# A state-space mixer whose running sums are loaded to all partitions from DRAM in place of a matmul with a triangle

## The chip, the cores and the metric

The kernel runs on one core of a Trainium2 chip. Its metric is the device time of one execution in microseconds (us). Five engines have queues of their own: PE (matmul; PEld is its weight load), DVE (VectorE), ACT (ScalarE), POOL (GpSimd) and SP (SyncE), which here issues nearly all DMAs. Each queue works strictly in order.

## The reference

Two layers of a diffusion trunk over 1024 latent and 128 context tokens, 1152 in all and thus nine blocks of 128. In each layer one projection feeds four mixers (state-space, neighbourhood attention, RWKV-7, differential attention); an output projection and an MLP follow. Only the state-space mixer is changed. For each head h, each direction and each block (chunk) of 128 tokens it computes

```python
la = (dt * A)                                   # 8 numbers per token: 2 directions x 4 heads
cs = jnp.cumsum(la, axis=-1)                    # running sums over the 128 tokens of the block
seg = jnp.where(tri, cs[..., :, None] - cs[..., None, :], -jnp.inf)
lmat = jnp.exp(seg).astype(dtype)
gmat = jnp.einsum('bclhn,bcshn->bhcls', Cc, Bc) * lmat
y_diag = jnp.einsum('bhcls,bcshp->bclhp', gmat, xdt)
```

So each block needs, for each of its eight (direction, head) pairs, a 128 x 128 tile cs[l] - cs[s]: cs[s] is a scalar per partition, and cs[l] is a row that must stand on all 128 partitions.

## The kernel before

Features lie on partitions, tokens along the free axis. The input projection is a row of calls of `proj` (feature-major, three chunks of 384 tokens, each chunk a product of 24 matmuls, three per k) and `proj_tm` (token-major, a product of 24 matmuls per block). Every large product is made of three fp32r matmuls per k (L99, L100, L101, in `mm3`), into PSUM tiles `psd` of which there are two.

In a layer the code is written in this order (L1477 to L1516): `proj` for the state-space mixer's four tiles and `proj_tm` for its z and dt; then `ssd` (the state-space mixer, L414); then nine further `proj` (the inputs of RWKV) and `proj_tm` for the values of the neighbourhood attention (its evacuations are L282, its stores to DRAM L283, its last store L287); then `rwkv_prep` (L595), which convolves the nine RWKV tiles and writes them back to DRAM; then `rwkv_open` and the first part of RWKV (`rwkv_first`, L777, called u00 here); then, in the pool `qk`, eight `proj_qk` and one more `proj_tm`.

The framework lists the instructions of each engine by a schedule of its own, by readiness and by priority: `rwkv_prep` has priority 1000, so its instructions are put as early as their data and their memory allow. Tiles come from pools that lie as stacks from the left and the right end of a partition's memory. A new pool that lies on the bytes of an older one waits until the older one's tiles are done with. The pools that matter:

- `sd_big` and `sd_tmp`, left: the tiles of `ssd`. They are given back when `ssd` is done.
- `rp`, left, right above `sd_tmp`: the tiles of `rwkv_prep` (`u` twice, `x0` to `x3`, each 1152 wide, `st` twice).
- `stg`, right: three buffers `st` of 384 columns, through which every `proj` and `proj_tm` goes to DRAM up to L287.
- `m1`, right, layer 0 only: the tiles of the modulation (`mod`, `junk`), a sum by DVE that runs beside the projections.
- `qk`, right, opened after `rp` is closed; it lies on the bytes of `rp`. `proj_qk` evacuates its products to it.

Within `ssd` the loop over blocks (L527) makes for each direction d a PSUM tile `cp`: for each head the column la of the block, broadcast to 128 columns, times the triangle `ctri[d]` (L560), which puts the running sums on all partitions. DVE subtracts the block's own sums from it into `Md` (L563), ACT takes the exponential (L565), DVE multiplies with the products of B and C (L566), and PE multiplies with the inputs (L572). PSUM tiles of `ssd` come from three buffers (`psr` twice, `psx`).

Before the loop the same running sums of all blocks and directions are already made once, as rows of 72 partitions (`cr`, L477 to L480); they are transposed to `cs`, the scalars per partition.

Of the kernel before, what the change touches and what calls it, by code (L numbers as in the profile page):

```python
# [8 lines left out]
F32 = mybir.dt.float32  # L9
# [10 lines left out]
NB = T // 128  # L20
# [14 lines left out]
def bcast_in(ap, n):  # L35
    return ap.unsqueeze(len(ap.shape)).to_broadcast(list(ap.shape) + [n])
# [58 lines left out]
def mm3(nc, ps, pairs):  # L95

    n = len(pairs)
    for i, ((ah, al), (bh, bl)) in enumerate(pairs):
        nc.tensor.matmul(ps, al, bh, start=i == 0, stop=False)  # L99
        nc.tensor.matmul(ps, ah, bh, start=False, stop=False)  # L100
        nc.tensor.matmul(ps, ah, bl, start=False, stop=i == n - 1)  # L101


def psd(env):

    env.turn += 1
    if env.wide and env.turn % 3 == 0:
        return psx(env)
    return ps2(env)
# [18 lines left out]
def psr(env):  # L128

    env.turnr += 1  # L130
    if env.turnr % 3 == 0:
        return psx(env)
    return env.ps_r.tile([128, 512], F32, tag="r", name="psr")
# [156 lines left out]
def residual(env, x, kt, c0, n, ps, g):  # L290
    for a0, m, cd in STREAMS:
        s0, s1 = max(a0, c0), min(a0 + m, c0 + n)
        if s1 > s0:
            env.nc.vector.scalar_tensor_tensor(out=x[:, kt, s0:s1], in0=ps[:, s0 - c0:s1 - c0], scalar=g[:, kt, cd:cd + 1],  # L294
                                               in1=x[:, kt, s0:s1], op0=ALU.mult, op1=ALU.add)
# [16 lines left out]

def out_proj(env, A, L, x, M, k0, g, first, xd=None):

    nc = env.nc
    nk = 6 - k0 if first else len(M)
    W = {}
    lo = k0 * 128

    def product(kt, c0, n):  # L320
        h, l = W[kt]
        ps = psd(env)
        mm3(nc, ps[:, :n], [((h[:, i * 128:i * 128 + 128], l[:, i * 128:i * 128 + 128]), (M[i][0][:, c0:c0 + n], M[i][1][:, c0:c0 + n])) for i in range(nk)])
        residual(env, x, kt, c0, n, ps, g)


    m = env.wcol // (nk * 128)
    order = []
    for a in range(0, 8, m):
        b = min(8, a + m)  # L330
        raw = env.wp.tile([128, env.wcol], F32, tag="raw", name="raw", bufs=1)[:, 0:(b - a) * nk * 128]
        nc.sync.dma_start(out=raw.rearrange("p (k x) -> p k x", k=b - a), in_=A["w_out"][L, a:b, :, lo:lo + nk * 128].rearrange("k p x -> p k x"))
        h, l = split(env, raw)
        for k in range(a, b):
            W[k] = h[:, (k - a) * nk * 128:(k - a + 1) * nk * 128], l[:, (k - a) * nk * 128:(k - a + 1) * nk * 128]
        if first:
            if a == 0:
                M = M()

            for k in (0, 1) if a == 0 else range(a + 1, min(b + 1, 8)):  # L340
                nc.vector.tensor_copy(x[:, k, 0:1], (l if a else M[-1][1])[:, 0:1].bitcast(F32))
                nc.sync.dma_start(out=x[:, k], in_=xd[:, k])
            for k in range(a, b):
                for c0, n in CH3:
                    product(k, c0, n)
    if not first:
        for c0, n in CH3:
            for kt in range(8):
                product(kt, c0, n)
# [64 lines left out]
def ssd(env, ctx, src, zdt, par, rows, st0, yout, stout):  # L414
    tc, nc, C = env.tc, env.nc, env.const
    big = ctx.enter_context(tc.tile_pool(name="sd_big", reuse_waits="tile", bufs=1))
    tp = ctx.enter_context(tc.tile_pool(name="sd_tmp", reuse_waits="tile", bufs=2))
    PS = lambda: psr(env)
# [4 lines left out]
    ctri, ctri2 = [t[:, 0], t[:, 1]], t.rearrange("p a b -> p (a b)")  # L423
    nc.vector.tensor_scalar_mul(out=pt[:, 0:24], in0=pt[:, 0:24], scalar1=0.5)
    xt = big.tile([128, NB, 256], F32, name="xt")
    x = [None, None]
# [45 lines left out]
    la = big.tile([128, NB, 8], F32, name="la")  # L472
    nc.vector.scalar_tensor_tensor(out=la, in0=dt, scalar=-1.0, in1=bcast_mid(eA, NB), op0=ALU.mult, op1=ALU.mult)

    cs = big.tile([128, NB, 8], F32, name="cs")
# [2 lines left out]
    nc.tensor.matmul(pc[:, 0:72], C.ones, f(la), start=True, stop=True)  # L478
    cr = tp.tile([72, 256], F32, tag="ze", name="cr")
    nc.scalar.activation(out=cr, in_=pr[0:72, 0:256], func=AF.Copy)  # L480
    for d in range(2):
        nc.tensor.transpose(pq[:, d * 72:d * 72 + 72], cr[:, d * 128:d * 128 + 128], C.ident[0:72, 0:72])
    for d in range(2):
# [12 lines left out]
    h4 = lambda a: a.rearrange("p (h x) -> p h x", h=4)  # L496
# [30 lines left out]
    for b in range(NB):  # L527
        zt = tp.tile([128, 256], F32, tag="zt", name="zt")
        nc.sync.dma_start(out=zt, in_=zdt[:, b, 0:256])
        ze = tp.tile([128, 256], F32, tag="ze", name="ze")  # L530
        nc.scalar.activation(out=ze, in_=zt, func=AF.Tanh, scale=0.5)
        nc.vector.tensor_scalar(out=ze, in0=ze, scalar1=0.5, scalar2=0.5, op0=ALU.mult, op1=ALU.add)
        nc.gpsimd.tensor_tensor(out=zt, in0=zt, in1=ze, op=ALU.mult)

        gp = [PS(), PS()]
        for g in range(2):
            w = slice(g * 64, g * 64 + 64)
            cb = x[3][w, b * 128:b * 128 + 128]
            nc.tensor.matmul(gp[g][:, 0:128], x[2][w, b * 128:b * 128 + 128], cb, start=True, stop=True)
            for d in range(2):  # L540
                nc.tensor.matmul(gp[g][:, 128 + d * 128:256 + d * 128], cb, Sin[w, d, b], start=True, stop=True)
        Gm = []
        for d in range(2):
            G = tp.tile([128, 256], F32, tag="Gm", name="Gm")
            for g in range(2):
                nc.vector.tensor_tensor(out=G[:, g * 128:g * 128 + 128], in0=gp[g][:, 0:128], in1=ctri[d], op=ALU.mult)
            Gm.append(G)
        t = tp.tile([128, 512], F32, tag="t", name="t")
        t4 = t.rearrange("p (d g h x) -> p d g h x", d=2, g=2, h=2)
        for g in range(2):  # L550
            for d in range(2):
                nc.vector.tensor_tensor(out=t4[:, d, g], in0=gp[g][:, 128 + d * 128:256 + d * 128].rearrange("p (h x) -> p h x", h=2),
                                        in1=bcast_in(ecs[:, b, d * 4 + g * 2:d * 4 + g * 2 + 2], 64), op=ALU.mult)
        M = []
        xd = tp.tile([128, 2, 256], F32, tag="xd", name="xd")
        for d in range(2):
            nc.gpsimd.tensor_tensor(out=h4(xd[:, d]), in0=h4(xt[:, b]), in1=bcast_in(dt[:, b, d * 4:d * 4 + 4], 64), op=ALU.mult)
            cp = PS()
            for h in range(4):
                nc.tensor.matmul(cp[:, h * 128:h * 128 + 128], la[:, b, d * 4 + h:d * 4 + h + 1].to_broadcast([128, 128]), ctri[d], start=True, stop=True)  # L560
            Md = tp.tile([128, 512], F32, tag="Md", name="Md")
            for h in range(4):
                nc.vector.tensor_scalar(out=Md[:, h * 128:h * 128 + 128], in0=cp[:, h * 128:h * 128 + 128], scalar1=cs[:, b, d * 4 + h:d * 4 + h + 1], scalar2=0.0,  # L563
                                        op0=ALU.subtract, op1=ALU.min)
            nc.scalar.activation(out=Md, in_=Md, func=AF.Exp)  # L565
            nc.vector.tensor_tensor(out=Md.rearrange("p (g h l) -> p g h l", g=2, h=2), in0=Md.rearrange("p (g h l) -> p g h l", g=2, h=2),  # L566
                                    in1=Gm[d].rearrange("p (g l) -> p g l", g=2).unsqueeze(2).to_broadcast([128, 2, 2, 128]), op=ALU.mult)
            M.append(Md)
        yp = PS()
        for h in range(4):  # L570
            for d in range(2):
                nc.tensor.matmul(yp[:, h * 64:h * 64 + 64], M[d][:, h * 128:h * 128 + 128], xd[:, d, h * 64:h * 64 + 64], start=d == 0, stop=d == 1)  # L572
        y = tp.tile([128, 256], F32, tag="y", name="y")
        nc.gpsimd.tensor_tensor(out=h4(y), in0=h4(xt[:, b]), in1=bcast_in(rb[:, 16:20], 64), op=ALU.mult)
        nc.gpsimd.tensor_tensor(out=t[:, 0:256], in0=t[:, 0:256], in1=t[:, 256:512], op=ALU.add)
        nc.gpsimd.tensor_tensor(out=y, in0=y, in1=t[:, 0:256], op=ALU.add)
        nc.vector.tensor_tensor(out=y, in0=y, in1=yp[:, 0:256], op=ALU.add)
        nc.gpsimd.tensor_tensor(out=xt[:, b], in0=y, in1=zt, op=ALU.mult)
        nc.scalar.activation(out=t[:, 0:256], in_=xt[:, b], func=AF.Square, accum_out=ss[:, 0, b:b + 1])
# [804 lines left out]
def kernel(ctx: ExitStack, tc: tile.TileContext, A: dict, O: dict):  # L1384
# [54 lines left out]
    for L in range(DEPTH):  # L1439
# [40 lines left out]
        proj_tm(env, A["w_in_tm"][L, 0], H, 264, zdt)  # L1480
        sx = ExitStack()
        ssd(env, sx, PF[0:4], zdt, A["ssd_par"][L], A["ssd_rows"][L], A["st_ssd"][L], Y[0:2], O["st_ssd"][L])
        for j in (10, 11, 12, 6, 4, 8, 7, 5, 9):
            proj(j)
# [248 lines left out]
```

## Time and profile before

| what | us |
|---|---|
| median of 3 runs (lowest to highest) | 4233.19 (4231.91 to 4238.97) |
| the profiled execution, its own time | 4236.38 |
| its span, first to last instruction | 4234.6 |
| PE busy in the span | 4062.3 (96%) |
| DVE busy | 2498.9 (59%) |
| ACT busy | 1524.2 (36%) |
| POOL busy | 1104.4 (26%) |

Start with the share of PE: it is busy for nearly the whole span, so what matters is where it works, where it idles, and what it would do instead. A layer's part of interest lies at 180 to 660 us (layer 0) and at 2275 to 2720 us (layer 1). The timelines and the chain of waits are read by start time; the lines name the place in the code. A busy time of PE counts the pipelined matmuls with their drains, so that the step from one start to the next, and not the length of a record, is what one matmul costs. One fp32 matmul leaves two records.

### The profile page before, as it was taken

How to read it: one execution, taken by the hardware profiler on the slowest of the kernel's cores; microseconds unless marked ns; L12 is line 12 of the kernel's file. 1: busy time of each engine (PE TensorE's matmuls, PEld its weight loads, DVE VectorE, ACT ScalarE, POOL GpSimd, SP SyncE). 2: the span in 40 equal slices, each digit the busy share in tenths (PEclk: the TensorE clock that was granted, in tenths of full speed). 3: DMA queues.
4: the chain of work that ended last, by engine and by line, in shares of the span. 5: the costliest groups of instructions: out<-in, count | busy, mean ns of one | idle time of the engine just before them, and what ended most of it. 6: DMA issues, size and time to landing. Idle time of an engine off the chain costs nothing.

```text
span 4234.6 us, 69159 instructions
## 1 busy us (share of the span) xinstructions
PE 4062.3 (96%) x27394; PEld 3722.1 (88%) x27394; DVE 2498.9 (59%) x5734; ACT 1524.2 (36%) x2896; POOL 1104.4 (26%) x866
## 2 busy tenths in 40 slices
PE   8899889999989999999999999899999999999999
PEld 5889877777779999999998998778777999999999
DVE  4896747678675894333345756576877463333333
ACT  4333325556553212211243233355566241111111
POOL 2243340223133221111232433302322331211111
PEclk9999989989999999999999998999889999999999
DMA  6663343322221451111134333543221301111111
GB/s 196 199 199 112 121 133 76 84 64 68 54 96 54 145 169 60 40 46 40 41 110 147 119 127 95 143 97 83 41 60 46 135 26 40 43 42 40 45 41 70
DMA packets 222707, 375.74 MB, mean 89 GB/s; under 512 B 100960, under 2 KB 155760, under 8 KB 221360
## 3 DMA queue, kind: packets, MB, share of 16 engines
q1 hardware_dynamic: 222320, 371.31, 29.2%
q8 instruction: 216, 3.54, 0.4%
q14 instruction: 107, 0.88, 0.1%
q0 software_dynamic: 64, 0.02, 0.0%
HBM read 285.33 MB, written 86.42 MB: 88 GB/s over the span
## 4 chain that ended last, share of the span: by engine, by line
PE 77%; DVE 11%; DMA 5%; issue 2%; SPq 2%; ACT 2%; POOL 1%; DVEq 0%; ACTq 0%; POOLq 0%
PE psd L101 12%; PE psd L99 12%; PE psd L100 12%; PE tps L1141 5%; PE psx L101 5%; PE psx L99 5%; PE psx L100 5%; PE tps L1129 3%; PE S L1347 2%; DVE junk L162 2%; PE psd L938 1%; DVE tm L867 1%; PE psd L958 1%; PE psd L930 1%; DMA K<-scr 1%
## 5 line engine op out<-in xcount | busy, mean ns | idle before, releaser
L84 POOL TENSOR_TENSOR wl<-raw,wh 128x1024 fp32r<-128x1024 f32 (+3 forms) x200 | 474.2, 2372 | 1543.1 <-ACT wh L82 1520.5
L82 ACT ACTIVATE wh<-raw 128x1024 fp32r<-128x1024 f32 (+3 forms) x200 | 205.9, 1031 | 793.8 <-PE psd L101 672.7
L294 DVE SCALAR_TENSOR_TENSOR x<-psd,md,x 128x384 f32<-128x384 f32 (+2 forms) x442 | 212.5, 504 | 349.5 <-PE psd L101 346.0
L101 PE MATMUL psd<-fl,wh 128*128 128x384 f32 x992 | 335.2, 338 | 0.0
L99 PE MATMUL psd<-fh,wl 128*128 128x384 f32 x992 | 334.7, 337 | 0.0
L100 PE MATMUL psd<-fh,wh 128*128 128x384 f32 x992 | 334.6, 337 | 0.0
L99 PE MATMUL psd<-h2h,wl 128*128 128x384 f32 x816 | 283.5, 348 | 9.1 <-ACT st L262 6.2
L1141 PE MATMUL tps<-pT,V 128*64 128x128 f32 (+1 forms) x2144 | 287.8, 284 | 4.5 <-ACT pT L1136 3.7
L100 PE MATMUL psd<-h2h,wh 128*128 128x384 f32 x816 | 282.7, 347 | 0.0
L101 PE MATMUL psd<-h2l,wh 128*128 128x384 f32 x816 | 281.3, 346 | 0.0
L1141 PEld LDWEIGHTS tps<-pT,V 128*64 128x64 f32 (+1 forms) x2144 | 239.1, 141 | 36.2 <-issue 22.8
L379 DVE TENSOR_TENSOR fl<-s,fh 128x384 fp32r<-128x384 f32 x192 | 209.1, 1090 | 97.4 <-ACT fh L378 97.0
L1136 ACT ACTIVATE pT<-tps 128x512 f32<-128x512 f32 (+3 forms) x368 | 166.3, 475 | 173.6 <-PE tps L1129 160.6
L99 PE MATMUL psd<-h0h,wl 128*128 128x384 f32 x592 | 207.5, 350 | 0.8 <-ACT qx L1098 0.6
L377 DVE SCALAR_TENSOR_TENSOR s<-psd,r 128x384 f32<-128x384 f32 x128 | 71.2, 556 | 231.2 <-ACT r L376 230.8
L99 PE MATMUL psd<-h1h,wl 128*128 128x384 f32 x592 | 205.3, 347 | 2.4 <-ACT h1h L244 2.0
L100 PE MATMUL psd<-h0h,wh 128*128 128x384 f32 x592 | 204.9, 346 | 0.0
L100 PE MATMUL psd<-h1h,wh 128*128 128x384 f32 x592 | 204.3, 345 | 0.0
L101 PE MATMUL psd<-h0l,wh 128*128 128x384 f32 x592 | 203.8, 346 | 0.0
L101 PE MATMUL psd<-h1l,wh 128*128 128x384 f32 x592 | 202.2, 343 | 0.1
L294 DVE SCALAR_TENSOR_TENSOR x<-psx,md,x 128x384 f32<-128x384 f32 (+2 forms) x198 | 103.4, 538 | 160.6 <-PE psx L101 160.2
L1353 ACT ACTIVATE e<-e,st 128x1280 f32<-128x1280 f32 x144 | 180.5, 1253 | 47.4 <-DVE st L1352 40.6
(613 smaller groups left out, 11021.3 us busy)
## 6 DMA issues: line engine op xcount, KB each, us to landing
raw<-in_w_ff_dram SPq DMA_DIRECT2D x128, 512.0 KB
mod<-in_w_mod_dram SPq DMA_DIRECT2D x80, 512.0 KB
raw<-in_w_in_fm_dram SPq DMA_DIRECT2D x42, 512.0 KB
scr<-st SPq DMA_DIRECT2D x78, 192.0 KB
scr<-x SPq DMA_DIRECT2D x26, 576.0 KB
K<-scr SPq DMA_DIRECT2D x32, 352.0 KB
K<-scr SPq DMA_DIRECT2D x64, 176.0 KB
u<-scr SPq DMA_DIRECT2D x18, 576.0 KB
```

Of the source, the lines that this page charges most:

```text
L82: nc.scalar.activation(out=h[:, :n], in_=raw, func=AF.Copy)
L84: nc.gpsimd.tensor_tensor(out=l[:, :n], in0=raw, in1=h[:, :n].bitcast(F32), op=ALU.subtract)
L99: nc.tensor.matmul(ps, al, bh, start=i == 0, stop=False)
L100: nc.tensor.matmul(ps, ah, bh, start=False, stop=False)
L101: nc.tensor.matmul(ps, ah, bl, start=False, stop=i == n - 1)
L162: nc.vector.scalar_tensor_tensor(out=junk, in0=w[:, i * 512:i * 512 + 512], scalar=0.5, in1=parts[c * 2 + i], op0=ALU.mult, op1=ALU.mult, ...
L294: env.nc.vector.scalar_tensor_tensor(out=x[:, kt, s0:s1], in0=ps[:, s0 - c0:s1 - c0], scalar=g[:, kt, cd:cd + 1], in1=x[:, kt, s0:s1], op0 ...
L379: nc.vector.tensor_tensor(out=fl[j][:, c0:c0 + n], in0=s, in1=fh[j][:, c0:c0 + n].bitcast(F32), op=ALU.subtract)
L1129: nc.tensor.transpose(pp[0:n, i * 128:i * 128 + 128], e[:, o:o + n], C.ident)
L1136: nc.scalar.activation(out=pT[0:g[i][1], i * 128:j * 128], in_=pp[0:g[i][1], i * 128:j * 128], func=AF.Copy)
L1141: nc.tensor.matmul(out, V[0:n, vb], parts[k // 4][0:n, k % 4 * 128:k % 4 * 128 + 128], start=k == 0, stop=k == len(kt) - 1)
L1353: nc.scalar.activation(out=e[:, :N], in_=e[:, :N], func=AF.Exp, scale=-1.0, bias=m, accum_out=st[:, 6:7] if c else s0)
```

## The change

The rows `cr` of running sums, which are there already, are stored to a DRAM tile `crd`, and each block loads its eight rows of 128 sums from it, broadcast to all 128 partitions, in two DMAs (one per direction) into a tile `cb`. The matmuls of L560 and their PSUM tile are gone. The subtraction works in place on `cb`, which then takes the part of `Md`. `Md` was a tile of 512 columns with two buffers, one tile per direction; `cb` is a tile of 2 x 512 columns with two buffers, one tile per block.

```diff
     cr = tp.tile([72, 256], F32, tag="ze", name="cr")
     nc.scalar.activation(out=cr, in_=pr[0:72, 0:256], func=AF.Copy)
+    crd = env.dram([NB, 8, 256])
+    nc.sync.dma_start(out=crd.rearrange("b x l -> (b x) l"), in_=cr)
...
         M = []
+
+        cb = tp.tile([128, 2, 512], F32, tag="Md", name="cb")
+        for d in range(2):
+            nc.sync.dma_start(out=h4(cb[:, d]), in_=crd[b, d * 4:d * 4 + 4, d * 128:d * 128 + 128].unsqueeze(0).to_broadcast([128, 4, 128]))
...
-            cp = PS()
+            Md = cb[:, d]
             for h in range(4):
-                nc.tensor.matmul(cp[:, h * 128:h * 128 + 128], la[:, b, d * 4 + h:d * 4 + h + 1].to_broadcast([128, 128]), ctri[d], start=True, stop=True)
-            Md = tp.tile([128, 512], F32, tag="Md", name="Md")
-            for h in range(4):
-                nc.vector.tensor_scalar(out=Md[:, h * 128:h * 128 + 128], in0=cp[:, h * 128:h * 128 + 128], scalar1=cs[:, b, d * 4 + h:d * 4 + h + 1], scalar2=0.0,
+                nc.vector.tensor_scalar(out=Md[:, h * 128:h * 128 + 128], in0=Md[:, h * 128:h * 128 + 128], scalar1=cs[:, b, d * 4 + h:d * 4 + h + 1], scalar2=0.0,
                                         op0=ALU.subtract, op1=ALU.min)
```

The tile doubles `Md`'s memory: `sd_tmp` grows by 4096 bytes per partition, and everything above it on the left moves up. In the built program before, `rp` ends at byte 118,776, and `stg` begins at byte 121,440. After, `rp` ends at byte 122,872, so its last tiles lie on the first buffer of `stg`.

The order of instructions moves with it. Line numbers after are three higher than before from `rwkv_prep` on. On the SP queue of layer 0 before, the parameters of `rwkv_prep` (`rpar`) and its first two tiles (`u`) stand among the stores of the projections (L263) and ahead of the first weights of the neighbourhood values:

```order
L525 DMA out_st_ssd_dram<-fin 128x128 x2
L263 DMA scr_198<-st 128x384
L159 DMA mod<-in_w_mod_dram 128x1024
L263 DMA scr_198<-st 128x384 x2
L599 DMA rpar<-in_rw_par_dram 128x41
L606 DMA u<-scr_201 128x1152
L606 DMA u<-scr_202 128x1152
L91 DMA raw<-in_w_in_tm_dram 128x1024
L263 DMA scr_196<-st 128x384
L529 DMA zt<-scr_212 128x256
```

After, the same loads (L602, L609) stand behind the last store of the neighbourhood values (L287), which is the last reader of `stg`:

```order
L283 DMA scr_213<-st 128x256
L287 DMA out_nat_v_dram<-st 128x256
L91 DMA raw<-in_w_in_fm_dram 128x1024
L602 DMA rpar<-in_rw_par_dram 128x41
L609 DMA u<-scr_201 128x1152
L609 DMA u<-scr_202 128x1152
L91 DMA raw<-in_w_in_fm_dram 128x1024
L609 DMA u<-scr_203 128x1152
L619 DMA scr_221<-x_3397 128x1152
```

So the whole of `rwkv_prep` has moved behind the projections and behind `ssd`; layer 1 has the same order. On PE of layer 0 before, the small products of `rwkv_prep` (L633, L662, L651) stand one by one among the projections' matmuls, as here:

```order
L99 MATMUL psd<-wh,h1l 128x256
L633 MATMUL psm<-pack,sq 128x2 x9
L560 MATMUL psr<-ctri,la 128x128 x4
L100 MATMUL psd<-wh,h1h 128x256
L560 MATMUL psr<-ctri,la 128x128 x4
L101 MATMUL psd<-wl,h1h 128x256
```

After, all of them (L636, L654, L665) and the products of u00 (L794, L804, L813, L848) stand in one unbroken stretch, behind the first two chunks of the first `proj_qk` and ahead of its third (the last row here); L794 stands just ahead of the first row:

```order
L804 MATMUL psr<-pack,lw 128x130 x3
L636 MATMUL psm<-pack,sq 128x2 x9
L804 MATMUL psr<-pack,lw 128x130 x3
L804 MATMUL psx<-pack,lw 128x130 x3
L813 MATMUL psr<-adn,up 128x384 x2
L813 MATMUL psx<-adn,up 128x384
L665 MATMUL psm<-pack,st 64x128 x18
L654 MATMUL psm<-x_3427,pack 128x384 x3
L848 MATMUL psr<-A,B 64x64 x32
L848 MATMUL psx<-A,B 64x64 x4
L636 MATMUL psm<-pack,sq 128x2 x9
L665 MATMUL psm<-pack,st 64x128 x18
```

What was spread over the projections is now in one piece between two products of the same `proj_qk`. On the SP queue the loads of `qk` (`qkpar`) have kept their place behind the last store of `rwkv_prep` (`bo`).

## Rows read from the trace of the kernel before

**Rows 1.** chain of waits, layer 1, 2270 to 2530 us: start us, us, what

```profile
...
2347.10 0.89 PE psx L560 x8
2348.34 2.12 PE psm L662 x36
...
2403.53 2.23 PE psm L633 x18
...
2428.05 1.94 PE psm L651 x6
...
```

**Rows 2.** instructions of line 560: ns min/median/max, first and last start

```profile
...
L560 PE MATMUL psr<-ctri,la x192: 270/275/421, 265.9 to 2462.5; 128*128 128x128 f32 x192
...
L560 PE MATMUL psx<-ctri,la x96: 270/275/376, 255.6 to 2465.3; 128*128 128x128 f32 x96
...
```

**Rows 3.** windows of layer 1: PE, PEld, DVE, ACT, POOL busy; PEclk, DMA share, GB/s

```profile
...
2420.00:2500.00 80.00, 80.00 (x578) 77.30 (x578) 40.95 (x106) 27.06 (x64) 29.90 (x27) 1.00 0.34 117
...
```

**Rows 4.** timeline of the SP queue, layer 0: start us, us, what

```profile
...
269.01 0.42 SPq L599 DMA_DIRECT2D rpar<-in_rw_par_dram  x1
...
374.34 0.32 SPq L616 DMA_DIRECT2D scr<-bo  x1
...
379.32 0.42 SPq L287 DMA_DIRECT2D out_nat_v_dram<-st  x1
...
```

**Rows 5.** timeline of the SP queue, layer 1, first load of rwkv_prep

```profile
...
2277.94 0.32 SPq L606 DMA_DIRECT2D u<-scr  x1
...
```

**Rows 6.** timeline of ACT, layer 1, the same load

```profile
...
2281.80 1.25 ACT L609 ACTIVATE x<-u,rpar 128x1152 f32<-128x1152 f32 x1 [4.47 <-DMA u<-scr]
...
```

**Rows 7.** timeline of DVE, layer 1, first convolution and one step of rsqrt

```profile
...
2283.09 1.99 DVE L611 SCALAR_TENSOR_TENSOR x<-u,rpar,x 128x1023 f32<-128x1023 f32 x2 [0.75 <-ACT x L609]
2285.00 1.89 DVE L612 SCALAR_TENSOR_TENSOR x<-u,rpar,x 128x1023 f32<-128x1023 f32 x2
...
2340.25 0.18 DVE L45 SCALAR_TENSOR_TENSOR st<-st 128x18 f32<-128x18 f32 x1
...
```

**Rows 8.** groups of DVE, 268 to 460 us: busy us, mean ns, idle before

```profile
...
L641 DVE SCALAR_TENSOR_TENSOR nk<-x,rnk,psm 128x384 f32<-128x384 f32 x6 | 3.6, 605 | 1.6 <-PE psm L662 1.6
...
L652 DVE TENSOR_TENSOR bo<-x,psm 128x384 f32<-128x384 f32 x6 | 3.2, 547 | 1.1 <-PE psm L651 1.0
...
L645 DVE SCALAR_TENSOR_TENSOR x<-x,rpar,x 128x1152 f32<-128x1152 f32 x2 | 2.8, 1402 | 0.0
...
L792 DVE TENSOR_TENSOR lw<-psr,w0b 128x384 f32<-128x384 f32 x2 | 1.1, 558 | 4.8 <-PE psr L791 4.7
...
```

**Rows 9.** groups of DVE, 2698 to 2716 us

```profile
...
L850 DVE TENSOR_TENSOR B<-a,k 128x1152 f32<-128x1152 f32 x1 | 1.4, 1387 | 0.0
...
L848 DVE TENSOR_TENSOR Ti<-psr,pack 64x512 f32<-64x512 f32 x2 | 1.4, 688 | 0.0
...
```

**Rows 10.** instructions of tile D: ns min/median/max, first and last start, forms

```profile
...
L868 DVE TENSOR_REDUCE D<-tm x248: 136/416/1152, 472.4 to 3076.5; 72x1 f32<-72x1 f32 x4, 72x3 f32<-72x9 f32 x4, 72x5 f32<-72x25 f32 x4, 72x7 f32<-72x49 f32 x4
...
```

**Rows 11.** chain of waits, layer 0, 180 to 470 us

```profile
...
427.37 1.53 PE psr L791 x12
...
```

**Rows 12.** groups of PE, 2698 to 2716 us

```profile
...
L845 PE MATMUL psr<-A,B 64*64 64x64 f32 x40 | 2.2, 297 | 0.0
...
```

**Rows 13.** timeline of PE, layer 0: two matmuls of a projection, nine apart

```profile
...
253.81 0.34 PE L100 MATMUL psd<-h0h,wh 128*128 128x384 f32 x1
...
255.39 0.34 PE L100 MATMUL psd<-h1h,wh 128*128 128x384 f32 x1
...
```

**Rows 14.** windows of PE, layer 0: busy, PEclk, DMA share, GB/s

```profile
...
308.00:312.00 4.00, 4.00 (x19) 0.50 0.49 157
...
```

**Rows 15.** waits of PE, 460 to 680 us: us in total, times, longest

```profile
...
PE psm L1066 <- DVE qf L1059: 10.7, 3, 5.6
...
```

**Rows 16.** instructions of line 563

```profile
...
L563 DVE TENSOR_SCALAR Md<-psr,cs x96: 334/341/351, 270.2 to 2467.5; 128x128 f32<-128x128 f32 x96
...
```

**Rows 17.** DMA packets in 2698 to 2716 us

```profile
...
DMA packets 4021, 4.05 MB, mean 225 GB/s; under 512 B 3316, under 2 KB 3316, under 8 KB 4018
...
```

## What the change was predicted to do

> **What bounds the kernel now.** I read the page's busy shares first, then the table of windows over the two stretches in which `ssd` stands, then the chain of waits there, then the timelines of SP, ACT and DVE for `rwkv_prep`. In the windows the reader is to see that PE does not rest while `ssd` and `rwkv_prep` run: in 2420 to 2500 us it is busy for all 80 us [rows 3]. The chain there runs through PE, and the products that the change removes are links of it: a group of four running-sum products (eight records) holds it for 0.89 us [rows 1]. `rwkv_prep`, though, is no link as a whole: it hides. In layer 0 its parameters are asked for at 269.01 us and its last store (`bo`) goes out at 374.34, ahead of the last store of the neighbourhood values at 379.32 [rows 4]. So PE has projections to do for as long as `rwkv_prep` lasts, and its end meets the end of the projections. That coincidence is what the change touches.
>
> **The products removed.** L560 left 192 + 96 = 288 records [rows 2], 36 groups of eight, 18 per layer. At 0.89 us each that is 32 us of PE in all, 16 per layer. PE is the bound there, so I take all of it as a gain, before what follows.
>
> **The edits that I cost at nothing.** The store of `cr` and the first loads of `cb` stand before the loop, with the chunk states of nine blocks still to be made on PE. The later loads of `cb` wait for the products of the block two before, and the projections fill PE in between; they cost nothing while the pair lands before its block's turn. The trace has no such load. Nearest are two rows: a 576 KB load reaches ACT 3.86 us after its issue (2281.80 less 2277.94) [rows 5, 6], and in 2698 to 2716 us, where the engines of DMA were never idle, 4021 packets took 18 us, 72 ns of one of 16 engines each [rows 17]; the 512 rows of 512 bytes in a 256 KB load would be 2.3 us. If nothing hid a pair once in two blocks, it would cost 3.86 + 2 x 2.3 = 8.5 us, four times a layer, 34 us per layer; the other end is zero, and I take zero, because of the two buffers, and keep 34 for the upper end. The subtraction took 0.34 us from PSUM [rows 16]; from SBUF, in place, I cannot see it being slower, and DVE is half idle in layer 1 (40.95 of 80 us) [rows 3]: nothing.
>
> The Trainium skill ("DMA: Bandwidth & Descriptors", section Bandwidth) speaks against such loads: it wants 1 MiB or more per DMA for three quarters of the peak. Its fit of a fixed 2.0 us plus bytes over 436 GB/s (SWDGE there, SP here) would give an estimate of 2.6 us for a 256 KB load and 5.2 for a pair in a row, against 8.5 from the rows; by either I leave the term at zero, and no run here shows such a load yet.
>
> **What is moved: `rwkv_prep`.** This is the term that decides. `rp` now lies on `stg`, and the order shows what follows: SP issues `rpar` and the first `u` only after L287, in both layers, and the stretch of small products on PE stands ahead of the third chunk of the first `proj_qk`. That chunk must also wait for another reason: `proj_qk` evacuates into `qk`, which lies on `rp`; so PE can fill the two `psd` and then has only the small products until the last `bo` is stored. `rwkv_prep` no longer lies beside the projections, but behind them. Queued behind its loads on SP are the loads of `qk`; behind its small products on PE, all of `proj_qk`.
>
> How long does it last alone? On DVE, in order, with the u00 work that stands between:
>
> - head, from the issue of `u` to DVE: 2283.09 - 2277.94 = 5.2 us [rows 5, 7];
> - nine convolutions of 2286.89 - 2283.09 = 3.8 us: 34 us [rows 7];
> - two rounds of rsqrt, 12 small instructions at 0.18 us [rows 7], 4.4 us; six nk at 0.605, two products at 1.40, six bo at 0.547 [rows 8]: 3.6 + 2.8 + 3.3; together 14 us;
> - u00 ahead of the last `bo`: three of 0.558 [rows 8], four 1152 wide at about 1.4, six of Ti of which four take 0.69 [rows 9], and some two dozen of the smallest steps of the block solve, which I put at 0.2 (its reduction has a minimum of 0.136 and a median of 0.416) [rows 10]: 1.7 + 5.6 + 3.3 + 5 = 16 us;
> - tail, the last store of `bo` until it has landed, as long as a load to ACT: 3.9 us [rows 5, 6].
>
> That is 73 us. Ahead of it stand the last store of the values until it has landed, some 4 us by the same rows, and its evacuation: 78 us from the end of the last product of the values until PE may go on. From this comes off what PE still does: two chunks of 24 matmuls at a step of (255.39 - 253.81) / 9 = 0.176 us [rows 13], 8.4 us; the small products of `rwkv_prep`, twice 2.23 + 2.12 + 1.94 = 12.6 us [rows 1]; those of u00, 18 records of L791 at 1.53 / 12 [rows 11] are 2.3, L801 and L810 about 4 by the same step, and 72 of L845 at 2.2 / 40 [rows 12] are 4: 10 us. The small ones had their time among the projections before, so as they fall into the gap now they count against it. Idle added: 78 - 8.4 - 12.6 - 10 = 47 us per layer.
>
> Bounds: at its shortest, without u00 between and with the head, the convolutions, the 14 and the tail alone, 57 + 5 us of gap and 31 us of idle. At its longest, as long as in layer 0 now, where it shares DVE with `ssd` and the modulation: 374.34 - 269.01 = 105 us [rows 4], 110 of gap, 79 of idle. I take 47.
>
> **After the gap.** PE comes back from sparse work. The granted clock of 308 to 312 us is 0.50, the lower of the two levels (1.2 GHz), right after a stretch in which PE stood still several times [rows 14]; if the level lasts twice that stretch, 8 us, it costs 4 us, which I add per layer (0 to 8). The Trainium skill ("TensorE: Matmul & The Clock Gate", section What's actually happening) has the same two levels, with the lower one as the state after idleness; by it the stretch of sparse products would run at the lower level too, which costs nothing there, and the trace agrees in the one row quoted. On the other side, with u00 done early, DVE has less to do while `proj_qk` runs. PE waited 10.7 us for its normalisation in layer 0 [rows 15]; I take 4 us per layer as given back, 0 to 10.
>
> **Sum.** Per layer 47 + 4 - 16 - 4 = 31 us, 62 for both. The profiled execution took 4236.38 us (span 4234.6 and some 2 us around it), 3 above the median of the runs, 4233.19. So 4298 on that execution, 4295 against the median; I say 4296.
>
> **Rivals.**
>
> - A, the removed products win and the move costs nothing: 4233 - 32 = 4201. For it: PE is the bound at 80 of 80 us [rows 3]. Against it: PE's order has no other work to put into the gap. Chance 4%.
> - B, the gap is real but short, and the gains eat it: 31 us of idle, no loss by the clock, 10 given back: 31 - 16 - 10 = +5 per layer at the most favourable, 4243; with a shorter convolution (DVE free of everything else) it could come down to no change. Chance 9%, of which 4 lie within 0.2%, 1 below, and 4 above.
> - C, slower by much more: the chain of `rwkv_prep` is as long as in layer 0 now, or the loads of `cb` come late as well. 79 + 4 - 16 = 67 per layer, 134, gives 4367; with 34 for the loads on top, up to 4435. For it: SP is in order, and within `rwkv_prep` loads now stand behind stores that wait (the reload of `wt` stands behind the store it reads, ahead of later `u`); `x3` has one buffer, used three times per round, with a store of some 4 us each. Against it: 105 us were needed while DVE was shared. Chance 19%.
>
> **How the numbers follow.** The forecast has 68%: 4296, its own range 4255 to 4345. The whole range of 4245 to 4365 leaves out A, most of B and the far part of C, together about 2 in 10. About 0.2%, 8 us, is what a measurement of this kernel can tell from no change. Faster by more than that: A with the small part of B, 5%; within it: 4%; slower: the rest, 91%.
>
> **What would show it.** In the profile after: no L560; PE busy less by some 32 us, and two gaps on PE of 70 to 80 us in which it does only small products, one per layer, each beginning two chunks after the last neighbourhood value product and ending when the last `bo` is stored, with the chain of waits on DVE (L614, L615) and DMA (`u`, `x`, `nk`, `bo`) inside; the clock at the lower level right after. Each step is wrong if: L575 waits for DVE or for `cb` by more than a few us per layer (the loads are late); the gap is under 55 or over 95 us (the length of `rwkv_prep`); or PE's waits for `qf` stay at 10.7 us (nothing given back). The forecast as a whole is wrong if `u` is loaded before L287, or if PE finds `psd` free and goes on with `proj_qk` inside the gap.

## The result, and the profile after

The changed kernel took 4305.47 us (median of 4 runs, 4303.45 to 4312.27) beside 4232.55 us of the kernel before: ratio 1.0174, 95% interval 1.0161 to 1.0187. It is slower by 73 us; 4296 was forecast, slower. The profiled execution took 4303.45 us, its span 4301.7. Two rows of its page: the busy time of PE with its records, and the DMA traffic.

```profile
...
PE 4043.8 (94%) x27106; PEld 3704.3 (86%) x27106; DVE 2504.6 (58%) x5734; ACT 1526.0 (35%) x2896; POOL 1097.4 (26%) x866
...
DMA packets 241881, 385.30 MB, mean 90 GB/s; under 512 B 101560, under 2 KB 174936, under 8 KB 240536
...
```

The 288 records of L560's products [rows 2] are gone (27394 before), but PE's busy time fell by 18.5 us and not by 32, and its idle time (span less busy) rose from 172 to 258 us.

Where, SP's timeline of layer 0 shows (start us, us, instruction), the answer to [rows 4]:

```profile
...
368.36 0.42 SPq L287 DMA_DIRECT2D out_nat_v_dram<-st  x1
...
369.96 0.43 SPq L602 DMA_DIRECT2D rpar<-in_rw_par_dram  x1
370.44 0.91 SPq L609 DMA_DIRECT2D u<-scr  x2
...
454.38 0.34 SPq L619 DMA_DIRECT2D scr<-bo  x1
454.77 0.42 SPq L1499 DMA_DIRECT2D qkpar<-in_qk_par_dram  x1
...
```

`rwkv_prep`'s parameters were asked for at 269.01 us, now at 369.96, right behind the last store of the values. In layer 1 it is the same. The windows of the changed kernel (length, PE busy and its records, granted clock, DMA share, GB/s) show what PE does meanwhile; the first two run from the last product of the values to the first of `proj_qk`'s third chunk, in either layer:

```profile
...
367.20:453.10 85.90, 47.47 (x285) 0.62 0.60 210
2470.90:2558.00 87.10, 48.61 (x284) 0.64 0.57 199
...
370.00:375.00 5.00, 5.00 (x30) 1.00 0.97 304
375.00:380.00 5.00, 0.92 (x6) 0.84 0.41 152
380.00:400.00 20.00, 6.04 (x27) 0.50 0.79 279
400.00:420.00 20.00, 16.17 (x75) 0.59 0.54 196
420.00:440.00 20.00, 9.47 (x93) 0.59 0.64 221
440.00:450.00 10.00, 3.96 (x37) 0.67 0.30 112
450.00:456.00 6.00, 6.00 (x20) 0.71 0.20 80
456.00:460.00 4.00, 4.00 (x29) 1.00 0.93 281
...
```

PE works off two chunks at 1.00 until 375 us, is idle for 38 us of the gap, does its small products mostly at the lower level of the clock (0.50 is 1.2 GHz; 0.50 to 0.67 in the rows of 380 to 450 us), and is back at 1.00 by 456 us. The chain of waits through the SSD and the gap (start us, us, what), first one of the loads of the sums, then pieces of `rwkv_prep`:

```profile
...
322.31 3.17 DMA cb<-scr
...
325.51 1.25 DVE cb L566 x3
...
370.44 5.98 DMA u<-scr
...
381.45 4.38 DMA u<-scr
...
399.80 3.63 PE psm L636 x18
...
436.56 3.84 DMA scr<-Ti
440.45 3.36 DMA D<-scr
...
449.71 2.91 PE psm L654 x4
...
```

The eighteen products of L636 took 2.23 us before [rows 1] and 3.63 here, at half the clock. At the end of the gap ACT takes the first chunk of `proj_qk` out of its `psd`, and 15 us later PE begins the third, which needs one of the two `psd`:

```profile
...
437.70 0.49 ACT L1101 ACTIVATE qx<-psd 128x384 f32<-128x384 f32 x1 [4.99 <-DVE x L615]
...
453.11 0.83 PE L99 MATMUL psd<-h2h,wl 128*128 128x384 f32 x1
...
```

Of PE's waits in 180 to 700 us (line, what it waited for: us, times, longest) two answer to the prediction's last paragraph, and one is new:

```profile
...
PE psr L794 <- DMA wt<-scr: 15.7, 1, 15.7
PE psm L1069 <- DVE qf L1062: 11.3, 1, 11.3
...
PE psx L575 <- DVE cb L569: 1.0, 2, 0.7
...
```

`qf` is waited for as long as before [rows 15]; new is `wt`, which is loaded back behind its own store inside the gap. The loads of the sums hardly make PE wait at L575. But DVE, which stands between, waited for them, in both layers together (what it waited for: us, times):

```profile
...
  DMA cb<-scr: 9.1, 9
...
```

And the subtraction (ns min/median/max, first and last start) is faster from SBUF than from PSUM, 275 ns against the 341 of [rows 16]:

```profile
...
L566 DVE TENSOR_SCALAR cb<-cb,cs x144: 268/275/2460, 207.1 to 2428.7; 128x128 f32<-128x128 f32 x144
...
```

The Trainium skill ("VectorE: DVE Perf Modes", section Why PSUM operands drop a tier) has a PSUM operand lose the mode that reads one fp32 tensor by two ports; at its 0.96 GHz that is an estimate of 67 ns for 128 elements, and the trace agrees with 66.

### The profile page after: what moved, and what is told of

It reads as the page before. It is cut to its first block, busy times and chain, and to the rows that moved or that the text cites. A ratio compares the mean times of both kernels' runs of the same rounds, so it can differ in the third digit from the quotient of the medians.

```text
span 4301.7 us, 68719 instructions
## 1 busy us (share of the span) xinstructions
PE 4043.8 (94%) x27106; PEld 3704.3 (86%) x27106; DVE 2504.6 (58%) x5734; ACT 1526.0 (35%) x2896; POOL 1097.4 (26%) x866
## 4 chain that ended last, share of the span: by engine, by line
PE 75%; DVE 12%; DMA 7%; issue 2%; ACT 2%; SPq 2%; POOL 1%; DVEq 0%; ACTq 0%; POOLq 0%
PE psd L99 12%; PE psd L101 12%; PE psd L100 12%; PE tps L1144 5%; PE psx L101 5%; PE psx L99 4%; PE psx L100 4%; PE tps L1132 3%; PE S L1350 2%; DMA K<-scr 2%; DVE junk L162 2%; PE psd L941 1%; DVE tm L870 1%; PE psd L961 1%; DMA mod<-in_w_mod_dram 1%
```

## The experiments

Two theories. **Memory:** the loss is `rwkv_prep` held behind the projections, because `rp` lies on `stg`; the rest of the change costs nothing or gains. **Loads:** the loads of the sums, by their bytes, latency or place on SP's queue, make the loss.

**One tile for each direction** (the changed kernel; memory as before, the same loads).

```
-        cb = tp.tile([128, 2, 512], F32, tag="Md", name="cb")
...
-            Md = cb[:, d]
+            Md = tp.tile([128, 512], F32, tag="Md", name="Md")
+            nc.sync.dma_start(out=h4(Md), in_=crd[b, d * 4:...].unsqueeze(0).to_broadcast([128, 4, 128]))
```

> The running sums are loaded from DRAM as in the changed kernel, in the same number of transfers and bytes, but into one tile of 128 x 512 for each direction, taken when that direction is worked on; the tiles then take no more memory than before, rp ends at byte 118,776 again and no longer lies on stg. Memory theory (the loss is rwkv_prep held behind the last store of the value projection): the gap of 85 us near 368 us and its twin in layer 1 are gone, and what the change itself does is left, 32 us of products gone against nothing or little for the loads: 4200 to 4215 us. Loads rival (the loads of the sums, their packets or their place on SP's queue make the loss): the loads are all still there, so 4290 to 4310 us.

Measured 4231.19 us, ratio 0.9992 (0.998 to 1.0005). The gap is gone, and with it the loads as the cause of the 73 us, but the expected gain is missing.

**A pad of 4,096 bytes, and one of 2,048** (the kernel before).

```
+    pad = big.tile([128, 1024], F32, name="pad")    # 512 in the second
+    nc.vector.memset(pad[:, 0:1], 0.0)
```

> The kernel before, with nothing of the change but a tile of 4,096 bytes in sd_big that is written in one column and read by nobody; rp then ends at byte 122,872, as in the changed kernel, and lies on stg. Memory theory: rwkv_prep moves behind the last store of the value projection as in the changed kernel, and without the products' gain the time is the changed kernel's plus up to 32 us: 4320 to 4340 us, with an idle stretch of TensorE of about 80 us in each layer. Loads rival: nothing is loaded, so the time is that of the kernel before, 4225 to 4240 us.

> As the kernel with a pad of 4,096 bytes, but with 2,048: rp ends at byte 120,824, 616 bytes below stg. Memory theory: the loss is a step at the first shared byte and not a price for each byte, so the time is that of the kernel before, 4225 to 4240 us, with rpar loaded near 269 us. If memory cost by the byte, it would lie halfway, near 4275 us. Loads rival: 4225 to 4240 us too.

Measured 4320.69 us, ratio 1.0208 (1.0192 to 1.0223), and 4232.79, ratio 0.9997 (0.9983 to 1.0012). SP of layer 0, with 4,096 bytes:

```profile
...
361.25 0.42 SPq L287 DMA_DIRECT2D out_nat_v_dram<-st  x1
...
362.78 0.42 SPq L601 DMA_DIRECT2D rpar<-in_rw_par_dram  x1
...
```

and with 2,048:

```profile
...
270.78 0.42 SPq L601 DMA_DIRECT2D rpar<-in_rw_par_dram  x1
...
378.92 0.42 SPq L287 DMA_DIRECT2D out_nat_v_dram<-st  x1
...
```

A tile that nobody reads costs 88 us, one of half its size nothing: a step where the two areas meet. This shows the memory theory without any of the change's own work.

**One buffer of `xd`, or two of `stg`** (the changed kernel; two ways to part `rp` from `stg`).

```
-        xd = tp.tile([128, 2, 256], F32, tag="xd", name="xd")
+        xd = tp.tile([128, 2, 256], F32, tag="xd", name="xd", bufs=1)
```
```
-        env.stg = early.enter_context(tc.tile_pool(name="stg", reuse_waits="tile", bufs=3, side="right"))
+        env.stg = early.enter_context(tc.tile_pool(name="stg", reuse_waits="tile", bufs=2, side="right"))
```

> The changed kernel with one buffer of xd in place of two, which frees 2,048 bytes: rp ends at byte 120,824, below stg. The loads of the sums stay in their pairs, two blocks ahead of use as before. Memory theory: no gap, 4200 to 4220 us; within 10 us of the kernel with one tile for each direction, unless the one buffer of xd makes POOL or TensorE wait, which would show as waits at the products that read xd. Loads rival: 4290 to 4310 us.

> The changed kernel, tiles of the sums and all, with two buffers in stg in place of three: stg begins at byte 122,976, 104 bytes above the end of rp, and nothing else of memory differs. Memory theory: the gap of 85 us goes as it did with one buffer of xd, 4195 to 4225 us; the upper end if the store tiles of the projections now wait for one another. If the loss sat in the place of rp alone and not in what it shares with stg, the time stays at 4290 to 4310 us.

Measured 4199.01 us, ratio 0.9918 (0.9906 to 0.9931), and 4220.08, ratio 0.9965 (0.9952 to 0.9979). With one `xd`, SP asks for `rpar` early again:

```profile
...
282.57 0.49 SPq L602 DMA_DIRECT2D rpar<-in_rw_par_dram  x1
...
382.89 0.42 SPq L287 DMA_DIRECT2D out_nat_v_dram<-st  x1
...
```

Both take the loss away from either side of the border, and the first beats both kernels by more than its interval: 34 us under the kernel before, 106 under the changed one. That is 32 us under the kernel with one tile for each direction, where at most 10 were expected.

**Three tiles, one for each direction** (`bufs=3` for `Md` in the first experiment's kernel).

```
-            Md = tp.tile([128, 512], F32, tag="Md", name="Md")
+            Md = tp.tile([128, 512], F32, tag="Md", name="Md", bufs=3)
```

> The kernel with one tile of sums for each direction (4231 us) with three such tiles in place of two; rp ends at byte 120,824, below stg. Depth theory (with two tiles a load can start only when the tile of two directions ago has been read by TensorE, so that its 3 us, the subtraction and the exponential stand on the path): a third tile gives the 32 us back, 4195 to 4210 us. Rival (the time of that kernel comes from where the rest of the work falls in the attention stages and not from the loads): 4225 to 4240 us.

Measured 4209.92 us, ratio 0.9948 (0.9932 to 0.9965): 21 us better than with two tiles, as the depth theory had it; the last experiments show what that is worth.

**The transfers doubled** (the kernel with one `xd`).

```
             nc.sync.dma_start(out=h4(cb[:, d]), in_=crd[b, d * 4:...].unsqueeze(0).to_broadcast([128, 4, 128]))
+            nc.sync.dma_start(out=crx[b, d], in_=crd[b, d * 4:...].unsqueeze(0).to_broadcast([128, 4, 128]))
```

> The changed kernel with one buffer of xd (4199 us), and beside each load of the sums a second transfer of the same source, shape and queue into a DRAM tensor that nobody reads: the packets, the bytes read and the issues on SP's queue for the sums are doubled, no memory of the core is touched. If the loads are covered, as the sum took it: within 6 us of 4199. If the loads have a price on SP's queue or on the DMA engines, it comes on top once more: 36 issues of 0.4 us to 36 landings of 3.2 us, 4213 to 4314 us.

Measured 4283.77 us, ratio 1.012 (1.01 to 1.0139). It tells less than hoped: the extra transfers wait for no tile, so many of a layer's 18 ran at once and ahead of the projections' stores on SP, and `rpar` was asked for at 354.3 us in place of 282.6. It prices another order, with `rwkv_prep` late in layer 0, and not the loads.

**The products doubled** (the kernel before).

```
-            for h in range(4):
+            for h in (0, 1, 2, 3, 0, 1, 2, 3):
                 nc.tensor.matmul(cp[:, h * 128:h * 128 + 128], la[...], ctri[d], start=True, stop=True)
```

> The kernel before with each group of four products of the broadcast column issued twice into the same PSUM bank, 288 products more: 36 x 0.89 us, 32 us of TensorE's time. If TensorE's time in this stage is worth its full length, as the sum took it: 4233 + 32 = 4265 us (4255 to 4275). If the stage hides part of it behind VectorE's recurrence: 4235 to 4250 us, and the 34 us by which the kernel with one buffer of xd is faster do not all come from the products.

Measured 4255.02 us, ratio 1.0048 (1.003 to 1.0066): 22 us for 32 us of PE, with an interval of 13 to 28: at the lower edge of the first range.

**One transfer for both directions** (the kernel with one `xd`).

```
+    crc = env.dram([NB, 2, 512])
+    for d in range(2):
+        nc.sync.dma_start(out=crc[:, d].rearrange("b (h l) -> b h l", h=4), in_=crd[:, d * 4:d * 4 + 4, d * 128:d * 128 + 128])
...
-        for d in range(2):
-            nc.sync.dma_start(out=h4(cb[:, d]), in_=crd[b, d * 4:...].unsqueeze(0).to_broadcast([128, 4, 128]))
+        nc.sync.dma_start(out=cb.rearrange("p d l -> p (d l)"), in_=crc[b].rearrange("d l -> (d l)").unsqueeze(0).to_broadcast([128, 1024]))
```

> The changed kernel with one buffer of xd (4199 us), its sums laid in DRAM so that one transfer of 512 KB brings both directions of a block: 18 issues on SP's queue in place of 36, the same bytes, and two small transfers at the head of each layer that lay the sums so. If the loads are covered: 4193 to 4206 us. If their place on SP's queue has a price (the kernel with the loads doubled lost 85 us, but there rwkv_prep's loads had also moved behind 18 more issues): 4180 to 4195 us.

Measured 4206.28 us, ratio 0.9931 (0.9915 to 0.9947): no gain over the 36 issues in the whole. In the two stages that the change touches (table below) it is 14 us shorter, 787 against 801, so whether the loads' place on SP has a price stays open.

**The sums loaded once, and the same with `rp` on `stg`** (the changed kernel).

```
+    cbx = big.tile([128, 512], F32, name="cbx")    # 1024 in the second
+    nc.sync.dma_start(out=cbx[...], in_=crd[0, 0:4, 0:128].unsqueeze(0).to_broadcast([128, 4, 128]))
...
-            Md = cb[:, d]
+            Md = tp.tile([128, 512], F32, tag="Md", name="Md")
-                nc.vector.tensor_scalar(out=Md[...], in0=Md[...], ...
+                nc.vector.tensor_scalar(out=Md[...], in0=cbx[...], ...
```

> Loads left out: the sums of block 0 and its first direction are loaded once for each layer, and every block and direction subtracts from that one tile into tiles of 128 x 512, so the output is not the reference's. Products, subtractions and exponentials are as in the changed kernel, rp ends at byte 120,824, below stg. If the 35 loads of a layer that are left out were covered: 4195 to 4210 us, that of the kernels with the loads and a free rp (4199, 4210, 4220). If they cost what the kernel with two tiles of sums suggests: 4165 to 4190 us.

> As the kernel that loads the sums once, with 2,048 bytes more in sd_big, so that rp ends at byte 122,872 and lies on stg as in the changed kernel. Memory theory without a part of the loads: the changed kernel's time, 4295 to 4310 us, that is, the 15 us by which the changed kernel lies under the pad of 4,096 bytes are all that the products are worth where rwkv_prep is held back. If the loads lie in that stretch on the path: 32 us under the pad of 4,096 bytes, 4280 to 4292 us.

Measured 4227.38 us, ratio 0.9988 (0.9979 to 0.9998), and 4287.04, ratio 1.0123 (1.0104 to 1.0141). (A layer has 18 loads, of which 17 are left out; the 35 above is a slip.) The first lies outside both ranges. With two tiles and nearly no loads the time is near that with two tiles and all loads (4231): where `rwkv_prep` has its old place the loads are covered in the whole, though DVE waited 30.0 us for them in that kernel. The second landed in the range that gives the loads a part where `rwkv_prep` is held back: it is 18 us under the changed kernel and 34 under the pad of 4,096 bytes. The windows from the first product of the sums to the last product of the values, so ahead of the gap, show where (length, PE busy and its records, clock, DMA share, GB/s; layer 0, then layer 1). With the pad, so with the products:

```profile
...
195.00:360.11 165.11, 158.69 (x1082) 0.99 0.37 112
2316.70:2494.45 177.75, 177.75 (x1227) 1.00 0.20 65
...
```

without products and nearly without loads:

```profile
...
196.30:358.46 162.16, 151.64 (x997) 0.95 0.38 116
2288.50:2449.66 161.16, 161.11 (x1101) 1.00 0.26 81
...
```

and the changed kernel, without products and with all loads:

```profile
...
195.40:367.20 171.80, 158.63 (x1015) 0.94 0.47 143
2303.70:2470.90 167.20, 164.75 (x1101) 0.98 0.35 109
...
```

In layer 1 PE never rests with the pad, and without the products the stretch is 17 us shorter, where the sum had 16; in layer 0 it is 3. With all loads it is 10 and 6 us longer again, 16 together; of the 6, PE's idle time makes 2.4 and its busy time, at a mean clock of 0.98, the rest. The changed kernel's chain of waits has four loads of the sums in it, 3.94 and 3.17 us in layer 0 and two in layer 1:

```profile
...
2392.32 1.72 PE psr L575 x14
...
2394.47 5.78 DMA cb<-scr
...
2403.24 3.97 DMA cb<-scr
...
```

The first of the two went out when the products (L575) that had read its tile were through. So the loads did stand on the path: 17 us by the chain, for which DVE was idle for 9.1 us and otherwise had other work. But the kernel that loads once has tiles of another shape too, so it isn't shown that the loads alone make the difference.

**Four tiles, products kept** (the kernel before).

```
-            Md = tp.tile([128, 512], F32, tag="Md", name="Md")
+            Md = tp.tile([128, 512], F32, tag="Md", name="Md", bufs=4)
...
+        xd = tp.tile([128, 2, 256], F32, tag="xd", name="xd", bufs=1)
```

> The kernel before, products and all, with four tiles Md in place of two and one xd in place of two; rp ends at byte 120,824, below stg. Of the kernels without products and with rwkv_prep in its old place, those with two tiles of 128 x 512 took 4231 us (with loads) and 4227 (nearly without), those with three or four 4199 to 4220. Depth theory (the gain is that of more tiles in flight, and the products were worth little): 4200 to 4215 us with the products still there. Products theory (without them TensorE ends earlier, and the tiles only let it): 4225 to 4240 us.

Measured 4233.27 us, ratio 1.0002 (0.9992 to 1.0012). More tiles alone bring nothing, and leaving the products out with two tiles brings 2 to 6 us; the gain of 13 to 34 us in the whole time appears only with both.

**Where the differences sit.** I cut every profile at the first product of the sums' line (L477 before) and the last of L1086, the end of `proj_qk`: all that the change touches lies in these two stages, one per layer. The windows (columns as above) of the kernel before,

```profile
...
194.20:605.40 411.20, 384.92 (x2536) 0.93 0.43 139
2282.40:2681.30 398.90, 388.88 (x2610) 0.96 0.37 123
...
```

of the changed one,

```profile
...
195.40:637.40 442.00, 376.94 (x2408) 0.88 0.44 141
2303.70:2738.10 434.40, 382.62 (x2476) 0.90 0.38 123
...
```

of the pad of 4,096 bytes,

```profile
...
195.00:633.60 438.60, 385.49 (x2534) 0.90 0.40 127
2316.70:2766.00 449.30, 395.75 (x2630) 0.90 0.34 112
...
```

and of the one with one `xd`:

```profile
...
196.20:601.50 405.30, 367.58 (x2380) 0.91 0.47 149
2259.00:2654.40 395.40, 376.93 (x2492) 0.94 0.43 139
...
```

The sum of the two stages, and the rest of the span, of every kernel, in us:

| kernel | two stages | rest |
|---|---|---|
| before | 810 | 3425 |
| pad 2,048 | 809 | 3421 |
| four tiles, products kept | 817 | 3415 |
| products doubled | 845 | 3412 |
| pad 4,096 | 888 | 3427 |
| changed | 876 | 3425 |
| loads once, `rp` on `stg` | 859 | 3416 |
| one tile per direction, two | 798 | 3437 |
| one tile per direction, three | 782 | 3425 |
| one `xd` | 801 | 3398 |
| one `xd`, one transfer | 787 | 3423 |
| two `stg` | 807 | 3411 |
| loads once | 801 | 3430 |
| transfers doubled | 840 | 3438 |

The whole loss of the changed kernel is in the two stages: 66 us of the 67 between the spans. But the rest, in which no kernel changes a line, moves between 3398 and 3438 us. The order that the build writes out also changes there. Each row is one execution, and behind the second stage the kernels with the pad of 2,048 and with four tiles have PE's order of before unchanged and still took 1546 and 1547 us in place of 1553: so some 8 us come without any change of order. Of the 36 us by which the fastest kernel's span is shorter than before, 9 lie in the two stages and 26 in the rest; the 36 us between it and the first experiment's kernel lie in the rest altogether. Why deeper tiles and missing products together come with the better rest isn't settled.

## Why the prediction was right, and by how much its terms were off

- **`rwkv_prep` moves behind the last store of the values: right.** The timelines show the place; both pads, one `xd` and two `stg` show that the shared bytes decide it.
- **A gap of 78 us: 85.9 and 87.1.** The tail did not come as thought: PE takes up the third chunk at 453.11 us, when its own last products (L654) are through, before the last `bo` is even issued (454.38). Nor was it held by a full `psd`: ACT had emptied one by 438.2 us, right after DVE's last convolution (L615). What stood ahead of the third chunk was PE's own order. What is longer is the body. The nine convolutions took DVE 30.3 us and not 34, but loads of `u` stood in the chain with 5.98 and 4.38 us, the round trip of `Ti` and `D` with 7.2, and small products at half the clock.
- **47 us idle: 38.4 and 38.5.** The small products were put at their full-speed length, 22.6 us; at the lower level they filled 39 (47.5 less 8.4 for the two chunks). So the gap grew by 8 to 9 us and the idle share of it shrank. What counts is the gap less the work at full speed, 55 us per layer where 51 stood in the sum (47 and 4).
- **The clock, 4 us after the gap: the wrong place.** It was back at 1.00 by 456 us; its price lay inside, on the small products, where the prediction had the lower level cost nothing.
- **4 us per layer given back by a shorter wait for `qf`: not seen** (11.3 against 10.7 us in layer 0, 9.8 against 6.9 in layer 1).
- **The products, 32 us: nearly right where `rwkv_prep` is held back, too much where it is not.** With `rp` on `stg`, as in the changed kernel, the pad and the kernel that loads once differ by 29 us in the two stages (888 and 859). With `rp` free of `stg`, the kernels without products are 3 to 28 us faster (807 to 782 against 810), five of six by under 25 and three by 9 or 12. Doubled, they cost 35 there, so PE is the bound when work is added, but not for all of what is taken away. The row of 80 busy us [rows 3] was read as if it held for the whole SSD; a window of the kernel before, at the SSD's start in layer 0 (length, then PE, PEld, DVE, ACT and POOL busy, clock, DMA), says otherwise, with DVE busy for 19.76 of 20 us and PE for 18.99:

```profile
...
260.00:280.00 20.00, 18.99 (x123) 17.75 (x124) 19.76 (x57) 5.85 (x8) 8.47 (x6) 1.00 0.56 193
...
```

- **The loads at zero: right with `rp` free of `stg`, most likely not in the changed kernel.** With `rp` free and two tiles, the two stages take 798 us with the loads and 801 nearly without. The changed kernel takes 17 us more than the kernel that loads once with `rp` on `stg` (876 and 859), with four loads in its chain; that the difference is theirs alone isn't shown. Two buffers did not hide a load that could go out only when its tile had been read. It showed at DVE, and not at L575, where the prediction looked. Of rival C's 34 us per layer it is a quarter. The Trainium skill ("DMA: Bandwidth & Descriptors", section Anatomy of one DMA — SWDGE (gpsimd) path) has a fit by which a load of 256 KB is an estimate of 2.6 us; the four rows, on SP's queue, are longer (3.17 to 5.78).
- **Sum per layer +31: +31 and +36** (442.0 - 411.2 and 434.4 - 398.9). It came out because errors met. Step by step in the two stages, the place of `rwkv_prep` costs 78 us (888 - 810) where 94 stood (47 and 4 less 4, twice); the products give 29 (888 - 859) where 32 stood; and the loads, or what else parts those two kernels, take 17 (876 - 859) where nothing stood: 66 in place of 62. So the closeness of 4296 is in part luck. By other pairs the place costs 58 (859 - 801) or 75 (876 - 801). All of these are less than twice the 55 us of a gap: some came back outside the gap. Ahead of it, the stretch up to the last product of the values took 183.6 and 196.3 us before and 165.1 and 177.8 with the pad, 18.5 less in either layer, where the small products' 12.6 stood; where the rest came back isn't settled. Rival A's 4201 is near the fastest of the kernels in which nothing is moved (4199 to 4231), and even there the gain is mostly not by the products.

## What to carry to other kernels

A larger tile is paid for where the pools end, not where it is used: before a tile grows, look at which later pool then shares bytes with one still in use, because a step of 4,096 bytes cost more than the work it saved. Test it by a tile that nobody reads, and mend it by giving up a buffer elsewhere. And where an order is written anew at each build, read a gain from the stage that was edited: the rest alone moved by 40 us, 8 of them with PE's order unchanged in its last part.

## What the runs showed of the hardware

The granted clock was 0.50 in 380 to 400 us, where PE was busy for 6.04 of 20 us, and 1.00 again in 456 to 460, with `proj_qk` taken up at 453.11: the return cost little, the sparse stretch more, since L636 went from 2.23 to 3.63 us. A `u` of 576 KB that reached ACT 3.86 us after its issue before [rows 5, 6] stood in the chain with 5.98 us when it went out in 370 to 375 us with a second `u`, right behind a load of weights (369.58), with the DMA engines 0.97 busy. A load of sums of 256 KB stood in the chain with 3.17 to 5.78 us.
